# First stage of a hybrid decoder layer: order of loads, norm by token tile, rank of the modulation, place of the transposes

## The chip, the cores and the metric

One core of one Trainium2 chip runs the kernel. The metric is the device time of one execution in microseconds; less is better. The time before is 936.29 us, the median of three runs (935.62 to 937.29). Engines are named as in the profile: PE (TensorE), DVE (VectorE), ACT (ScalarE), POOL (GpSimd), SP (the queue that issues the loads).

## The reference, cut to what matters

512 tokens, width 1024, all in float32. The first stage of the layer computes a conditioned norm and projects it:

```python
mod = (jax.nn.silu(c) @ w_ada + b_ada)[:, None, :]
shift_a, scale_a, gate_a, shift_f, scale_f, gate_f = jnp.split(mod, 6, axis=-1)
h = rms_norm(x, attn_norm) * (1.0 + scale_a) + shift_a
(nq, nkc, nvc, nks, nvs, nkw, nvw, ngate,
 cq, ckv, kr, bgate) = jnp.split(h @ w_in, IN_OFFSETS, axis=-1)
```

Attention over compressed, selected and windowed keys, a second attention (MLA), an output projection and a gated MLP follow; the change leaves their code alone.

## The kernel before, in words

The width is cut into eight blocks `k` of 128 columns, the tokens into four tiles `t` of 128. Every float32 product is made of three matmuls: both operands are split into a high and a low part (`split`, L82: ACT rounds the high part at L83, DVE subtracts at L84), and `mm3` (L87) multiplies high by high, low by high and high by low. `wh`/`wl` are the parts of a weight piece, `hTh`/`hTl` those of the transposed, modulated `h`.

**First stage.** `x` comes in as eight loads (L417). The sum of squares of each half row (L434, L437) gives `rsx`, two token tiles at a time, through POOL (L135). `x_half(i)` scales half of the columns and transposes four blocks `k` into `xnT` (L453, L455). The conditioning vector is a matrix-vector product: `mod_acc(j)` loads eight pieces of `w_ada` (`ada`, 256 KB each, L467), which hold the shifts and the scales of two blocks (a pair `j`, `j+1`), and adds them up on DVE (`acc`, L120 and L122). `mod_cols(j)` sums `acc` over the partitions with two one-column matmuls (operand `onesr`) and makes the columns `mS` and `mA` (L477 to L480). `prep(k)` loads two pieces of `w_in` (408 and 384 columns, `wr`), splits them, and makes `h` of `xnT`, `mS` and `mA` on ACT (L507), then `hTh` and `hTl`. Block `k`'s step of the projection is then 12 matmuls of 408 columns into four banks (`psG`, `psG`, `psS`, `psS`) and 9 of 512 into `psO`, `psF` and a `psT`.

**Second stage.** The four banks of 408 columns are turned into gates (`gt`, `gates`) and a normalized `cqn` for each token tile (L548), which frees the bank. The same four banks and `psF` then take the projection of 320 + 128 further columns (`bB`, `bV1`), block by block. `psF` must first be read by the three instructions L573 to L575 (rotary embedding, output `a`). `X` are the split inputs of the compression, made of `kc`.

**Order.** A scheduler places the instructions on each engine by its own timeline, ranked by a priority (`tc.high_priority`); an engine then takes them in the order in which they stand. `tc.keep_in_program_order` (`pin`) fixes one. Tiles of one tag share a number of buffers (`BIG`, `BANKS`, `bufs`): a load or a matmul into a buffer waits until it has been read out. `W_PRIO` is the rank of the weight splits, `LATE` a list of which small late load goes with which block.

Of the kernel before, what the change touches and what calls it, by code (L numbers as in the profile page):

```python
# [10 lines left out]
F32 = mybir.dt.float32  # L11
# [22 lines left out]
LATE = (0, 1, 1, 1, 2, 2, 2, 3, 3, 4, 5, 6, 7, 8, 9, 9, 9)  # L34
X_ACT = ((0, 0, 1, 1), (1, 1, 1, 1))
# [3 lines left out]
def tile_hybrid_layer(  # L39
# [18 lines left out]
    W_PRIO = [-50]  # L58
# [37 lines left out]
    def raw_unit():  # L96
        return wp.tile([P, 512], F32, name="wr", tag="wr", bufs=5)

    @priority(lambda: W_PRIO[0])
    def load_w(segs, k0, kk, raw=None, tag=None):  # L100
        n = sum(g[2] for g in segs)
        assert kk * n <= 512
        raw = raw_unit() if raw is None else raw
# [5 lines left out]
        rv, hv, lv = (a[:, :kk * n].rearrange("p (k n) -> p k n", k=kk) for a in (raw, wh, wl))  # L109
        at = 0  # L110
        for src, c0, m in segs:
            dma(rv[:, :, at:at + m],
                src[k0 * P:(k0 + kk) * P, c0:c0 + m].rearrange("(k p) n -> p k n", p=P))
            at += m
        split(wh[:, :kk * n], wl[:, :kk * n], raw[:, :kk * n])
        return hv, lv

    def gemv_step(acc, w, k, init):
        if k == 0 and init:
            vec.tensor_scalar(acc, w, csil[:, 0:1], None, op0=ALU.mult)  # L120
        else:
            vec.scalar_tensor_tensor(acc, w, csil[:, k:k + 1], acc, op0=ALU.mult, op1=ALU.add)  # L122
# [286 lines left out]
    with tc.tile_pool(name="p1", bufs=1) as p1:  # L409
# [15 lines left out]
        vec.tensor_scalar(csil, csil, 0.5, None, op0=ALU.mult)  # L425

        ssh = sm.tile([P, NT, 2], F32, name="ssh")
        ssx = sm.tile([P, NT], F32, name="ssx")
        rsx = sm.tile([P, NT], F32, name="rsx")
        for t in range(NT):  # L430
            for i in range(2):
                if i:
                    scr = pj.tile([P, 512], F32, name="scr", tag="t2")
                    vec.tensor_tensor_reduce(scr, xt[t][i], xt[t][i], 1.0, 0.0, ALU.mult, ALU.add, ssh[:, t, i:i + 1])  # L434
                else:
                    scr = pj.tile([P, 512], F32, name="scr", tag="qg")
                    act.activation(scr, xt[t][i], AF.Square, accum_out=ssh[:, t, i:i + 1])  # L437
            if t % 2:
                t2 = slice(t - 1, t + 1)
                vec.tensor_add(ssx[:, t2], ssh[:, t2, 0], ssh[:, t2, 1])  # L440
                rstd(rsx[:, t2], ssx[:, t2], D, [P, 2])
        xnT = []

        def x_half(i):
            for t in range(NT):
                if X_ACT[i][t]:
                    act.activation(xt[t][i], xt[t][i], AF.Copy, scale=rsx[:, t:t + 1])
                else:
                    vec.tensor_scalar(xt[t][i], xt[t][i], rsx[:, t:t + 1], None, op0=ALU.mult)
            for k in range(4 * i, 4 * i + 4):  # L450
                tr = bank("T")
                for t in range(NT):
                    pe.transpose(tr[:, t * P:(t + 1) * P], xt[t][i][:, (k % 4) * P:(k % 4 + 1) * P], ident)  # L453
                xk = slot("KV", f"xnT{k}") if k < 6 else slot("KS", f"xnT{k}")[:, 0:512]
                act.activation(xk, tr, AF.Copy)  # L455
                xnT.append(xk)

        x_half(0)
# [3 lines left out]
        def mod_acc(j):  # L462
            if j % 2 == 0:
                acc = slot("U", "acc")
                for k in range(KD):
                    a = slot("ml", "ada")
                    dma(a.rearrange("p (s n) -> p s n", s=2),  # L467
                        w_ada[k * P:(k + 1) * P, 0:2 * D].rearrange("p (s n) -> p s n", s=2)[:, :, j * P:(j + 2) * P])
                    gemv_step(acc, a, k, True)
                for i in range(2):  # L470
                    ACC[j + i] = [acc[:, s * 256 + i * P:s * 256 + (i + 1) * P] for s in range(2)]

        def mod_cols(j):
            b = bank("T")
# [3 lines left out]
            bp = sm.tile([P, 1], F32, name="bp")  # L478
            vec.scalar_tensor_tensor(bp, b[:, 1:2], 1.0, colA[:, 24 + j:25 + j], op0=ALU.add, op1=ALU.add)
            vec.tensor_mul(mA[:, j:j + 1], bp, colA[:, 8 + j:9 + j])  # L480
# [11 lines left out]
        def late_load(i):  # L492
            for dst, src in late[LATE[i]:LATE[i + 1]]:
                tc.keep_in_program_order(dma(dst, src))

        bA = [bank("G"), bank("G"), bank("S"), bank("S")]
        bF = [bank("O"), bank("F"), None]
        wk = {}

        def prep(k):  # L500
            mod_acc(k)
            mod_cols(k)
            wk[k] = (load_w([(w_in, O_NG, 408)], k, 1, slot("cq", "wr1")),
                     load_w([(w_in, O_KC, 384)], k, 1, slot("cq", "wr2")))
            late_load(k)
            h = pj.tile([P, 512], F32, name="h", tag="t1")
            act.activation(h, xnT[k], AF.Identity, scale=mA[:, k:k + 1], bias=mS[:, k:k + 1])  # L507
            hh, hl = slot("hT", f"hTh{k}", F32R), slot("hT", f"hTl{k}", F32R)
            split(hh, hl, h)
            hTh.append(hh)  # L510
            hTl.append(hl)

        prep(0)
        x_half(1)
        for k in range(KD):
            if k + 1 < KD:
                prep(k + 1)
            if k == 0:
                bF[2] = bank("T")
            hh, hl = hTh[k], hTl[k]  # L520
            (w1h, w1l), (w2h, w2l) = wk[k]
            st, sp = k == 0, k == KD - 1
            for t in range(NT):
                ts = slice(t * P, (t + 1) * P)
                mm3(bA[t][:, 0:408], hh[:, ts], hl[:, ts], w1h[:, 0, :], w1l[:, 0, :], st, sp)
            for i in range(3):
                cs = slice(i * P, (i + 1) * P)
                mm3(bF[i], w2h[:, 0, cs], w2l[:, 0, cs], hh, hl, st, sp)

        tr = bank("T")  # L530
        pe.transpose(tr[:, 0:76], rowsB, ident[0:76, 0:76])
# [7 lines left out]
        for t in range(NT):  # L539
            b = bA[t]  # L540
            act.activation(gt[:, t, :], b[:, 0:24], AF.Tanh, scale=0.5)
            s1 = sm.tile([P, 1], F32, name="s1")
            sq = pj.tile([P, 512], F32, name="sq", tag="t2")
            act.activation(sq[:, 0:384], b[:, 24:408], AF.Square, accum_out=s1)
            r1 = sm.tile([P, 1], F32, name="r1")
            rstd(r1, s1, 384, [P, 1])
            cn = slot("ml", f"cqn{t}")
            vec.scalar_tensor_tensor(cn[:, 0:384], b[:, 24:408], r1, gcq, op0=ALU.mult, op1=ALU.mult)  # L548
            cqn.append(cn)
# [8 lines left out]
        for k in range(KD):  # L558
            wh, wl = load_w([(w_in, O_CKV, 320), (w_in, O_VC + P, P)], k, 1)
            late_load(KD + k)  # L560
# [4 lines left out]
            mm3(bV1, wh[:, 0, 320:448], wl[:, 0, 320:448], hTh[k], hTl[k], st, sp)  # L565

# [550 lines left out]
```

## Time and profile before

| what | value |
|---|---|
| median of three runs | 936.29 us |
| the profiled execution | 936.09 us |
| its span, first to last instruction | 934.1 us |
| PE, DVE, ACT busy | 900.9, 689.3, 511.0 us |
| mean granted TensorE clock | 0.998 |

The profiled execution lies 0.2 us under the median; 2.0 us of it lie outside the span. Times in the rows are microseconds from the span's start. The first projection matmul starts at 22.96, the first stage's last one ends at 63.39, the second stage's at 83.88.

### The profile page before, as it was taken

Reading aid. Unit: us, or ns where it says so; the run is one execution under the profiler, and the core shown is the slowest. Engines: PE = TensorE matmul, PEld = TensorE weight load, DVE = VectorE, ACT = ScalarE, POOL = GpSimd, SP = SyncE. Lnnn points to the kernel's source line nnn. Section 1 sums busy time; section 2 is a strip of 40 time slices with the busy share of each in tenths; the row PEclk is TensorE's granted clock in tenths of the full one; section 3 lists DMA queues with packets and bytes.
Section 4 is the critical chain, followed back from the end, with each engine's and each line's share of the span. In section 5 each row is a group of like instructions: output and inputs, shape, how many; then the busy total and the mean of one; then the engine's idle time right before and its main releaser. Section 6 shows DMA issues by size and latency. Waiting matters only on the chain.

```text
span 934.1 us, 14791 instructions
## 1 busy us (share of the span) xinstructions
PE 900.9 (96%) x5079; PEld 790.9 (85%) x5079; DVE 689.3 (74%) x1505; ACT 511.0 (55%) x1241; POOL 49.9 (5%) x57
## 2 busy tenths in 40 slices
PE   4899999999999999999999999999999999999998
PEld 3899888889899998889898889888888888888886
DVE  7967878798977779688877798797786766722423
ACT  5546868567675657558765764554444444422220
POOL 1000101011000001001011010000000000000000
PEclk9999999999999999999999999999999999999999
DMA  9934672542331263341214354363353333232421
GB/s 299 346 115 140 183 213 83 157 127 54 106 99 35 58 172 102 103 138 35 57 58 147 100 178 118 91 192 91 118 167 99 93 99 101 92 102 91 145 91 46
DMA packets 131682, 113.05 MB, mean 121 GB/s; under 512 B 7515, under 2 KB 110487, under 8 KB 131607
## 3 DMA queue, kind: packets, MB, share of 16 engines
q1 hardware_dynamic: 130838, 110.00, 39.4%
q0 software_dynamic: 768, 2.11, 0.7%
q8 instruction: 40, 0.66, 0.3%
q14 instruction: 36, 0.29, 0.1%
HBM read 109.98 MB, written 2.10 MB: 120 GB/s over the span
## 4 chain that ended last, share of the span: by engine, by line
PE 89%; DVE 4%; ACT 3%; DMA 3%; issue 1%; SPq 0%; DVEq 0%; ACTq 0%
PE psG L87 42%; PE psS L87 24%; PE psO L87 9%; PE psF L87 5%; PE psT L87 4%; PE psT L783 2%; DMA ada<-in_w_ada_dram 2%; DVE wl L84 1%; ACT Pt L760 1%; ACT wh L83 1%; ACT sq L223 1%; DMA x<-in_x_dram 1%; DMA wr<-in_w_in_dram 0%; DVE acc L122 0%; PE psT L808 0%
## 5 line engine op out<-in xcount | busy, mean ns | idle before, releaser
L83 ACT ACTIVATE wh<-wr 128x512 fp32r<-128x512 f32 (+3 forms) x304 | 187.1, 621 | 288.5 <-PE psS L87 104.2
L84 DVE TENSOR_TENSOR wl<-wr,wh 128x512 fp32r<-128x512 f32 (+3 forms) x304 | 203.3, 676 | 158.1 <-ACT wh L83 150.8
L87 PE MATMUL psG<-hTh,wh 128*128 128x512 f32 x192 | 76.5, 399 | 1.0 <-DVE qr L328 1.0
L87 PE MATMUL psG<-hTh,wl 128*128 128x512 f32 x192 | 76.3, 397 | 0.1
L87 PE MATMUL psG<-hTl,wh 128*128 128x512 f32 x192 | 76.3, 397 | 0.0
L87 PE MATMUL psS<-h2l,wh 128*128 128x512 f32 (+1 forms) x184 | 68.2, 371 | 0.0
L87 PE MATMUL psG<-h2h,wl 128*128 128x512 f32 (+1 forms) x184 | 68.2, 371 | 0.0
L87 PE MATMUL psG<-h2l,wh 128*128 128x512 f32 (+1 forms) x184 | 68.1, 371 | 0.0
L87 PE MATMUL psG<-h2h,wh 128*128 128x512 f32 (+1 forms) x184 | 68.1, 372 | 0.0
L87 PE MATMUL psS<-h2h,wl 128*128 128x512 f32 (+1 forms) x184 | 68.0, 371 | 0.0
L87 PE MATMUL psS<-h2h,wh 128*128 128x512 f32 (+1 forms) x184 | 68.0, 371 | 0.0
L760 ACT ACTIVATE Pt<-psS,nm 128x128 f32<-128x128 f32 (+2 forms) x96 | 51.3, 535 | 26.1 <-DVE nm L755 20.1
L122 DVE SCALAR_TENSOR_TENSOR acc<-wr,csil,acc 128x512 f32<-128x512 f32 x60 | 44.8, 747 | 2.9 <-DMA wr<-in_w_ada_dram 1.6
L84 DVE TENSOR_TENSOR PTl<-psT,PTh 128x384 fp32r<-128x384 f32 (+1 forms) x72 | 42.2, 598 | 6.4 <-ACT PTh L83 5.8
L83 ACT ACTIVATE PTh<-psT 128x384 fp32r<-128x384 f32 (+1 forms) x72 | 36.6, 530 | 16.5 <-PE psT L783 16.3
L87 PEld LDWEIGHTS psG<-hTh,wh 128*128 128x128 f32 x192 | 36.2, 188 | 7.6 <-PE psS L87 0.7
L87 PEld LDWEIGHTS psG<-hTh,wl 128*128 128x128 f32 x192 | 36.1, 188 | 7.2 <-DVE wl L84 0.5
L87 PEld LDWEIGHTS psG<-hTl,wh 128*128 128x128 f32 x192 | 36.1, 188 | 6.4
L87 PE MATMUL psG<-wh,hTh 128*128 128x256 f32 (+2 forms) x128 | 38.1, 308 | 3.6 <-ACT wh L83 2.2
L87 PEld LDWEIGHTS psG<-h2l,wh 128*128 128x128 f32 x184 | 34.7, 188 | 6.1
L87 PE MATMUL psG<-wl,hTh 128*128 128x256 f32 (+2 forms) x128 | 38.9, 305 | 0.9 <-DVE wl L84 0.9
L87 PEld LDWEIGHTS psG<-h2h,wh 128*128 128x128 f32 x184 | 34.6, 188 | 6.0
(452 smaller groups left out, 2515.1 us busy)
## 6 DMA issues: line engine op xcount, KB each, us to landing
wr<-in_w_up_dram SPq DMA_DIRECT2D x88, 256.0 KB, 2.9
wr<-in_w_ada_dram SPq DMA_DIRECT2D x64, 256.0 KB, 2.8
wr<-in_w_in_dram SPq DMA_DIRECT2D x48, 256.0 KB, 3.1
wr<-in_w_down_dram SPq DMA_DIRECT2D x44, 256.0 KB, 2.6
ada<-in_w_ada_dram SPq DMA_DIRECT2D x32, 256.0 KB, 5.6
wr<-in_w_o_dram SPq DMA_DIRECT2D x32, 256.0 KB, 3.0
wr<-in_w_in_dram SPq DMA_DIRECT2D x32, 128.0 KB, 2.9
wr<-in_cmp_k_w_dram SPq DMA_DIRECT2D x16, 256.0 KB, 3.3
```

What stands on the lines that cost most here:

```text
L83: act.activation(hi, src, AF.Copy)
L84: vec.tensor_sub(lo, src, f(hi))
L87: ins = pe.matmul(o, lhsT, rhs, start=start, stop=stop, skip_group_check=True)
L122: vec.scalar_tensor_tensor(acc, w, csil[:, k:k + 1], acc, op0=ALU.mult, op1=ALU.add)
L223: act.activation(sq[:, 0:n], b, AF.Square, accum_out=dst)
L760: act.activation(Pt[:, off[x2]:off[x2] + nt[x2]], Sb[x2], AF.Exp, bias=nm[:, x2:x2 + 1], scale=-1.0, accum_out=sums[:, x2:x2 + 1])
L783: pe.transpose(tr[:, e * P:(e + 1) * P], Pt[:, o:o + P], ident)
```

## The change

All loads of the first two stages are pinned in one order on SP: `x` token tile by token tile with the first pieces of `w_ada` between them, the rest of the first pair, `w_in` for blocks 0 and 1, the next pair, `w_in` for the next two blocks, and so on; the small late loads come after the last pair. Each token tile has its own norm, and seven of the eight sums of squares are on ACT. The first four blocks are transposed as their token tile is ready, into four banks (two `psT`, `psO`, `psF`); block 0 is modulated straight out of its bank. `mod_cols`, `x_tile`, `h_split` and the `cqn` loop are ranked 300; the steps are made in pairs. Two DVE instructions for `mA` become one. Cut to its core:

```diff
-LATE = (0, 1, 1, 1, 2, 2, 2, 3, 3, 4, 5, 6, 7, 8, 9, 9, 9)
-X_ACT = ((0, 0, 1, 1), (1, 1, 1, 1))
+LATE = (3, 4, 5, 6, 7, 8, 9, 9, 9)
...
-    W_PRIO = [-50]
+    W_PRIO = [300]
+    pin = tc.keep_in_program_order
...
+        at = 0
         for t in range(NT):
             for i in range(2):
-                dma(xt[t][i], x[t * P:(t + 1) * P, i * 512:(i + 1) * 512])
+                pin(dma(xt[t][i], x[t * P:(t + 1) * P, i * 512:(i + 1) * 512]))
+            for k in range(at, (0, 1, 2, 8)[t]):
+                load_ada(0, k)
+            at = (0, 1, 2, 8)[t]
+        for k in range(2):
+            load_in(k)
...
+        trx = [bank(tag) for tag in ("T", "T", "O", "F")]
+        @priority(lambda: 300)
+        def x_tile(t):
...
+            pool.tensor_tensor(rsx[:, t:t + 1], msx[:, t, 1:2], neghalf, op=ALU.pow)
+            vec.tensor_scalar(xt[t][0], xt[t][0], rsx[:, t:t + 1], None, op0=ALU.mult)
+            act.activation(xt[t][1], xt[t][1], AF.Copy, scale=rsx[:, t:t + 1])
+            for k in range(4):
+                pe.transpose(trx[k][:, t * P:(t + 1) * P], xt[t][0][:, k * P:(k + 1) * P], ident)
...
+        def mod_acc(j, held):
+            acc = slot("U", "acc")
+            for k in range(KD):
+                gemv_step(acc, ada[j, k], k, True, held and k == 0)
...
+            if k:
+                act.activation(h, xnT[k], AF.Identity, scale=mA[:, k:k + 1], bias=mS[:, k:k + 1])
+                split(hh, hl, h)
+            else:
+                act.activation(hh, trx[0], AF.Identity, scale=mA[:, 0:1], bias=mS[:, 0:1])
+                vec.tensor_scalar(h, trx[0], mA[:, 0:1], mS[:, 0:1], op0=ALU.mult, op1=ALU.add)
+                vec.tensor_sub(hl, h, f(hh))
...
+        for j in range(0, KD, 2):
+            if j + 2 < KD:
+                for k in range(KD):
+                    load_ada(j + 2, k)
+                for k in (j + 2, j + 3):
+                    load_in(k)
+                mod_acc(j + 2, True)
+            else:
+                late_load(-1)
...
+            if j + 2 == KD:
+                wB = [load_b(k, 2) for k in range(2)]
+            proj(j)
+            proj(j + 1)
+            if j + 2 < KD:
+                for k in (j + 2, j + 3):
+                    mod_cols(k)
...
+        with tc.high_priority(offset=300):
+            for t in range(NT):
+                b = bA[t]
```

What this makes of the engines' order is shown at three places. The first is DVE at the first modulation. Before:

```order
L122 SCALAR_TENSOR_TENSOR acc<-ada,csil,acc 128x512 x7
L84 TENSOR_TENSOR wl<-wr_232,wh 128x408
L120 TENSOR_SCALAR acc<-ada,csil 128x512
L84 TENSOR_TENSOR wl<-wr_238,wh 128x384
L477 TENSOR_TENSOR mS<-psT,colA 128x1
L479 SCALAR_TENSOR_TENSOR bp<-psT,colA 128x1
```

And of the change:

```order
L139 SCALAR_TENSOR_TENSOR acc<-ada,csil,acc 128x512 x4
L87 TENSOR_TENSOR wl<-wr_143,wh 128x408
L87 TENSOR_TENSOR wl<-wr_144,wh 128x384
L87 TENSOR_TENSOR wl<-wr_147,wh 128x408
L87 TENSOR_TENSOR wl<-wr_148,wh 128x384
L503 TENSOR_TENSOR mS<-psG,colA 128x1
L504 SCALAR_TENSOR_TENSOR mA<-psG,bp_158,colA 128x1
```

The first `mS` stood behind the two weight splits of block 0; it now stands behind those of blocks 0 and 1. The second place is PE where the modulation of later blocks is summed. Before, inside block 3's step:

```order
L87 MATMUL psS<-wh,hTl_424 128x408
L87 MATMUL psT<-onesr,acc 128x1 x2
L87 MATMUL psS<-wh,hTl_424 128x408
L87 MATMUL psO<-hTl_424,wh 128x512
L87 MATMUL psO<-hTh_423,wl 128x512
```

Of the change, between block 1 (`hTh_301`) and block 2 (`hTh_435`); it looks the same between blocks 3 and 4 and between 5 and 6:

```order
L92 MATMUL psF<-hTh_301,wl 128x512
L92 MATMUL psT<-hTl_302,wh 128x512
L92 MATMUL psT<-hTh_301,wl 128x512
L92 MATMUL psT<-onesr,acc 128x1 x4
L92 MATMUL psG<-wh,hTh_435 128x408
L92 MATMUL psG<-wl,hTh_435 128x408
```

The one-column matmuls have moved from inside a step to directly ahead of the step that needs them. The third place is DVE after the last block's `hTl`, where the banks of the first stage are read out. Before:

```order
L548 SCALAR_TENSOR_TENSOR cqn_718<-psG,r_714,qs_113 128x384
L132 TENSOR_SCALAR ms<-s_731 128x1
L573 TENSOR_TENSOR a_946<-psO,tabs 128x512
L548 SCALAR_TENSOR_TENSOR cqn_728<-psG,r_724,qs_113 128x384
L84 TENSOR_TENSOR wl<-wr,wh 128x448
L550 TENSOR_SCALAR gates<-gt 128x4x24
```

Of the change, with the first `cqn` (`cqn_720`) just ahead of the first row shown:

```order
L87 TENSOR_TENSOR wl<-wr,wh 128x448
L628 TENSOR_TENSOR gates<-gates,tabs 128x1
L149 TENSOR_SCALAR ms<-s_733 128x1
L149 TENSOR_SCALAR ms<-s_743 128x1
L652 TENSOR_TENSOR a_935<-psO,tabs 64x512
L653 TENSOR_TENSOR a_935<-psO,tabs 64x512
L608 TENSOR_SCALAR qcol<-colB 128x1
L609 TENSOR_SCALAR gcol<-colB 128x1
L87 TENSOR_TENSOR X<-colB,X 128x16x2
L624 SCALAR_TENSOR_TENSOR cqn_730<-psG,r_726,qs_113 128x384
L624 SCALAR_TENSOR_TENSOR cqn_740<-psS,r_736,qs_113 128x384
L624 SCALAR_TENSOR_TENSOR cqn_750<-psS,r_746,qs_113 128x384
```

The second to fourth `cqn` have moved from among the first `a` to behind all three of its instructions, two weight splits and most of the gates.

## Rows read from the trace of the kernel before

**Rows 1.** The page: busy time of each engine, and the chain of work that ended last by engine.

```profile
PE 900.9 (96%) x5079; PEld 790.9 (85%) x5079; DVE 689.3 (74%) x1505; ACT 511.0 (55%) x1241; POOL 49.9 (5%) x57
...
PE 89%; DVE 4%; ACT 3%; DMA 3%; issue 1%; SPq 0%; DVEq 0%; ACTq 0%
```

**Rows 2.** Busy time by stage. Columns: stretch, its length, then busy time and number of instructions of PE, PEld, DVE, ACT, POOL, the granted TensorE clock, the DMA share and GB/s.

```profile
0.00:22.96 22.96, 9.14 (x38) 6.75 (x38) 16.09 (x43) 13.79 (x27) 2.54 (x8) 1.00 0.92 298
22.96:63.39 40.43, 38.05 (x198) 34.85 (x197) 29.95 (x73) 21.17 (x46) 1.64 (x3) 1.00 0.79 258
63.39:83.88 20.49, 20.16 (x124) 18.89 (x123) 17.36 (x45) 11.31 (x26) 1.38 (x3) 1.00 0.36 102
...
104.00:136.00 32.00, 28.35 (x206) 26.10 (x205) 26.50 (x51) 21.71 (x54) 4.67 (x3) 0.95 0.70 202
```

**Rows 3.** PE in order of time in the first stage. Columns: start, duration, engine, line, operation, output and inputs, shape, count, and in brackets the idle time before and what ended it.

```profile
19.18 4.12 PE L453 MATMUL psT<-ident,x 128*128 128x128 f32 x16
22.96 0.69 PE L87 MATMUL psG<-wh,hTh 128*128 128x408 f32 x1
...
29.54 0.60 PE L87 MATMUL psT<-onesr,acc 128*128 128x1 f32 x4 [0.96 <-DVE bp L479]
...
34.38 0.34 PE L87 MATMUL psG<-wh,hTh 128*128 128x408 f32 x1
...
38.64 0.34 PE L87 MATMUL psG<-wh,hTh 128*128 128x408 f32 x1
...
41.35 0.50 PE L87 MATMUL psT<-onesr,acc 128*128 128x1 f32 x4
...
45.28 0.45 PE L87 MATMUL psG<-wh,hTh 128*128 128x408 f32 x1 [1.41 <-ACT hTh L83]
```

**Rows 4.** The loads: GB/s in slices of 1.25 us from 0 to 50 us, and the DVE instruction that waited for the twentieth load (the second pair's first `ada`).

```profile
GB/s 0 25 231 315 254 293 310 389 380 353 346 351 361 351 333 346 348 351 369 380 363 342 348 350 364 358 382 311 317 357 317 334 359 348 294 315 393 354 344 240
...
18.93 0.49 DVE L120 TENSOR_SCALAR acc<-ada,csil 128x512 f32<-128x512 f32 x1 [0.74 <-DMA ada<-in_w_ada_dram]
```

**Rows 5.** DVE and ACT in order of time: links of the chain from a modulation's sum to `hTh`, and one weight split of 384 columns.

```profile
18.13 0.51 ACT L83 ACTIVATE wh<-wr 128x384 fp32r<-128x384 f32 x1
...
43.77 0.80 ACT L507 ACTIVATE h<-xnT,mS,mA 128x512 f32<-128x512 f32 x1
44.59 0.63 ACT L83 ACTIVATE hTh<-h 128x512 fp32r<-128x512 f32 x1
...
53.80 0.82 ACT L507 ACTIVATE h<-xnT,mS,mA 128x512 f32<-128x512 f32 x1 [2.65 <-DVE mA L480]
```

**Rows 6.** DVE in order of time, first and second stage.

```profile
19.33 0.55 DVE L84 TENSOR_TENSOR wl<-wr,wh 128x384 fp32r<-128x384 f32 x1
...
41.92 0.15 DVE L477 TENSOR_TENSOR mS<-psT,colA 128x1 f32<-128x1 f32 x1
41.99 0.15 DVE L479 SCALAR_TENSOR_TENSOR bp<-psT,colA 128x1 f32<-128x1 f32 x1
...
53.54 0.16 DVE L480 TENSOR_TENSOR mA<-bp,colA 128x1 f32<-128x1 f32 x1
...
62.35 0.68 DVE L573 TENSOR_TENSOR a<-psO,tabs 128x512 f32<-128x512 f32 x1
62.95 0.61 DVE L548 SCALAR_TENSOR_TENSOR cqn<-psG,r,qs 128x384 f32<-128x384 f32 x1
63.47 0.61 DVE L84 TENSOR_TENSOR wl<-wr,wh 128x448 fp32r<-128x448 f32 x1
...
64.83 0.69 DVE L574 TENSOR_TENSOR a<-psO,tabs 64x512 f32<-64x512 f32 x1
...
71.20 1.98 DVE L84 TENSOR_TENSOR X<-kc,X 128x496 fp32r<-128x496 f32 x2
```

**Rows 7.** PE in order of time, second stage.

```profile
63.39 0.23 PE L531 MATMUL psT<-ident,rowsB 76*128 76x76 f32 x1
63.42 0.39 PE L87 MATMUL psG<-wh,hTh 128*128 128x320 f32 x1
63.65 0.31 PE L87 MATMUL psG<-wl,hTh 128*128 128x320 f32 x1
...
71.22 0.50 PE L87 MATMUL psF<-hTh,wh 128*128 128x512 f32 x1 [0.33 <-DVE a L575]
...
74.08 0.45 PE L87 MATMUL psG<-wh,hTh 128*128 128x320 f32 x2
...
83.65 0.39 PE L87 MATMUL psF<-hTh,wl 128*128 128x512 f32 x1
```

**Rows 8.** ACT in order of time, second stage.

```profile
73.42 0.58 ACT L83 ACTIVATE wh<-wr 128x448 fp32r<-128x448 f32 x1 [0.16 <-PE psF L87]
74.10 2.09 ACT L83 ACTIVATE X<-kc 128x496 fp32r<-128x496 f32 x2
```

**Rows 9.** Busy time and granted clock around 110 us, columns as in rows 2, and ahead of them the wait of PE there.

```profile
107.75 0.50 PE L87 MATMUL psG<-wh,hTh 128*128 128x256 f32 x2 [1.00 <-ACT wh L83]
...
108.00:110.00 2.00, 1.65 (x9) 1.44 (x9) 2.00 (x4) 2.00 (x3) 0.00 (x0) 0.73 0.35 87
110.00:112.00 2.00, 2.00 (x12) 2.00 (x11) 2.00 (x4) 2.00 (x9) 0.00 (x0) 0.50 0.73 224
112.00:114.00 2.00, 2.00 (x18) 2.00 (x18) 2.00 (x5) 1.15 (x3) 0.88 (x1) 0.92 0.03 8
```

More of the change, by code (lines that the diff above doesn't have):

```diff
@@ L108, in load_w, with gemv_step @@
             wl = wp.tile([P, 512], F32R, name="wl", tag="wl", bufs=4)
[L109 to L115, printed above, removed]
+        hv, lv = (a[:, :kk * n].rearrange("p (k n) -> p k n", k=kk) for a in (wh, wl))
+        split(wh[:, :kk * n], wl[:, :kk * n], raw[:, :kk * n], held)
         return hv, lv
[L118 removed]
+    def gemv_step(acc, w, k, init, held=False):
         if k == 0 and init:
[L120 removed]
+            ins = vec.tensor_scalar(acc, w, csil[:, 0:1], None, op0=ALU.mult)
+            if held:
+                pin(ins)
         else:
@@ L414, in tile_hybrid_layer, with load_ada, load_in @@
         dma(rowsA, vec_a)
+        ada, raws = {}, {}
+        G1, G2 = [(w_in, O_NG, 408)], [(w_in, O_KC, 384)]
+        def load_ada(j, k):
+            a = slot("ml", "ada")
+            pin(dma(a.rearrange("p (s n) -> p s n", s=2),
+                    w_ada[k * P:(k + 1) * P, 0:2 * D].rearrange("p (s n) -> p s n", s=2)[:, :, j * P:(j + 2) * P]))
+            ada[j, k] = a
+        def load_in(k):
+            raws[k] = [slot("cq", f"wr{i}") for i in range(2)]
+            for r, g in zip(raws[k], (G1, G2)):
+                load_raw(r, g, k, 1)
+        at = 0
         for t in range(NT):
             for i in range(2):
-                dma(xt[t][i], x[t * P:(t + 1) * P, i * 512:(i + 1) * 512])
+                pin(dma(xt[t][i], x[t * P:(t + 1) * P, i * 512:(i + 1) * 512]))
[4 more added lines that the diff above has]
+            load_in(k)
         tr = bank("T")
@@ L458, in tile_hybrid_layer @@
-        x_half(0)
-        ACC = {}
[L462 to L471, printed above, removed]
+            vec.tensor_scalar(msx[:, t, 0:1], ssh[:, t, 0:1], 1.0 / D, EPS, op0=ALU.mult, op1=ALU.add)
@@ L473, in mod_cols @@
+        ACC = {}
+        def mod_acc(j, held):
+            acc = slot("U", "acc")
+            for k in range(KD):
+                gemv_step(acc, ada[j, k], k, True, held and k == 0)
+            for i in range(2):
+                ACC[j + i] = [acc[:, s * 256 + i * P:s * 256 + (i + 1) * P] for s in range(2)]
+        @priority(lambda: 300)
         def mod_cols(j):
-            b = bank("T")
+            b = bank("G" if j < 2 else "T")
             for s in range(2):
@@ L477, in mod_cols, with x_keep, x_half1 @@
             vec.tensor_add(mS[:, j:j + 1], b[:, 0:1], colA[:, 16 + j:17 + j])
-            bp = sm.tile([P, 1], F32, name="bp")
-            vec.scalar_tensor_tensor(bp, b[:, 1:2], 1.0, colA[:, 24 + j:25 + j], op0=ALU.add, op1=ALU.add)
-            vec.tensor_mul(mA[:, j:j + 1], bp, colA[:, 8 + j:9 + j])
+            vec.scalar_tensor_tensor(mA[:, j:j + 1], b[:, 1:2], bp1[:, j:j + 1], colA[:, 8 + j:9 + j],
+                                     op0=ALU.add, op1=ALU.mult)
+        for t in range(NT):
+            x_tile(t)
+        mod_acc(0, False)
+        for j in range(2):
+            mod_cols(j)
+        xnT = [None]
+        def x_keep(k, tr):
+            xk = slot("KV", f"xnT{k}") if k < 7 else slot("KS", f"xnT{k}")[:, 0:512]
+            act.activation(xk, tr, AF.Copy)
+            xnT.append(xk)
+        def x_half1(k0, k1):
+            for k in range(k0, k1):
+                tr = bank("T")
+                for t in range(NT):
+                    pe.transpose(tr[:, t * P:(t + 1) * P], xt[t][1][:, (k % 4) * P:(k % 4 + 1) * P], ident)
+                x_keep(k, tr)
         rowsB = p1.tile([76, P], F32, name="rowsB")
@@ L492, in late_load, with w_split, h_split, load_b @@
         def late_load(i):
[L493 to L497, printed above, removed]
+            for dst, src in late[0 if i < 0 else LATE[i]:LATE[i + 1]]:
+                pin(dma(dst, src))
         wk = {}
[L500 to L505, printed above, removed]
+        def w_split(k):
+            wk[k] = [load_w(g, k, 1, r) for g, r in zip((G1, G2), raws[k])]
+        @priority(lambda: 300)
+        def h_split(k):
             h = pj.tile([P, 512], F32, name="h", tag="t1")
-            act.activation(h, xnT[k], AF.Identity, scale=mA[:, k:k + 1], bias=mS[:, k:k + 1])
             hh, hl = slot("hT", f"hTh{k}", F32R), slot("hT", f"hTl{k}", F32R)
-            split(hh, hl, h)
+            if k:
[5 more added lines that the diff above has]
+                vec.tensor_sub(hl, h, f(hh))
             hTh.append(hh)
             hTl.append(hl)
[L513 to L519, printed above, removed]
+        def load_b(k, held=0):
+            return load_w([(w_in, O_CKV, 320), (w_in, O_VC + P, P)], k, 1, held=held)
+        def proj(k):
             hh, hl = hTh[k], hTl[k]
@@ L528, in tile_hybrid_layer @@
                 mm3(bF[i], w2h[:, 0, cs], w2l[:, 0, cs], hh, hl, st, sp)
+        wB = []
+        for j in range(0, KD, 2):
[5 more added lines that the diff above has]
+                mod_acc(j + 2, True)
+            else:
+                late_load(-1)
+            if j == 0:
+                w_split(0)
+                h_split(0)
+                for k in range(1, 4):
+                    x_keep(k, trx[k])
+                w_split(1)
+                h_split(1)
+                x_half1(4, 8)
+                bA = [bank("G"), bank("G"), bank("S"), bank("S")]
+                bF = [bank("O"), bank("F"), bank("T")]
+            else:
+                for k in (j, j + 1):
+                    w_split(k)
+                    h_split(k)
+            if j + 2 == KD:
[5 more added lines that the diff above has]
+                    mod_cols(k)
         tr = bank("T")
-        pe.transpose(tr[:, 0:76], rowsB, ident[0:76, 0:76])
+        pin(pe.transpose(tr[:, 0:76], rowsB, ident[0:76, 0:76]))
         vec.tensor_copy(colB, tr[:, 0:76])
@@ L538, in tile_hybrid_layer @@
         cqn, ckvn = [], []
[L539 to L549, printed above, removed]
+        with tc.high_priority(offset=300):
+            for t in range(NT):
+                b = bA[t]
+                act.activation(gt[:, t, :], b[:, 0:24], AF.Tanh, scale=0.5)
+                s1 = sm.tile([P, 1], F32, name="s1")
+                sq = pj.tile([P, 512], F32, name="sq", tag="t2")
+                act.activation(sq[:, 0:384], b[:, 24:408], AF.Square, accum_out=s1)
+                r1 = sm.tile([P, 1], F32, name="r1")
+                rstd(r1, s1, 384, [P, 1])
+                cn = slot("ml", f"cqn{t}")
+                vec.scalar_tensor_tensor(cn[:, 0:384], b[:, 24:408], r1, gcq, op0=ALU.mult, op1=ALU.mult)
+                cqn.append(cn)
         vec.tensor_scalar(gates.rearrange("p g t -> p t g"), gt, 0.5, 0.5, op0=ALU.mult, op1=ALU.add)
```

72 lines of the change are left out of this document (37 added, 35 removed).

## The prediction

> **What bounds the kernel now.** I read the page first. PE is busy 96% of the span and the chain that ended last runs through PE for 89% of it [rows 1]: a gain has to come out of stretches where PE waits or starts late, and a loss is whatever makes PE wait anew. The change touches the first two stages, so I cut the span there [rows 2]. Up to 22.96 PE does only transposes and sums and the loads run at 298 GB/s; that is the one stretch where PE is late. From 22.96 to 63.39 PE is busy 38.05 of 40.43 us, and from 63.39 to 83.88 it is busy 20.16 of 20.49: both stages are already PE's. From 104 to 136 PE idles 3.65 us.
>
> Next I read PE in order of time [rows 3]. One block's step takes 4.26 us (34.38 to 38.64), eight take 34.1; the other 6.3 us of the stage are one-column sums and waits such as the 0.96 us at 29.54 and the 1.41 us at 45.28. So a new first stage can win by starting before 22.96, and by having less than 6.3 us beside its steps.
>
> **The start of the projection.** In both kernels the first pair's modulation rests on the same 17 loads (one small, eight of `x`, eight `ada`), 33 KB and sixteen times 262 KB, 4.23 MB, so mixing `x` and `ada` cannot bring its last piece earlier. What decides is what stands ahead of the first `mS` on DVE: now four weight splits, so four pieces of `w_in`, the last of which ends at 5.04 MB. Before, a load that ended at 4.93 MB was waited for until 18.93 [rows 4]; 0.11 MB more at 348 GB/s is 0.3 us, so it lands at 19.2. Then ACT's high part 0.51 [rows 5], DVE's low part 0.55, `mS` and 0.07 later `mA` for 0.16 [rows 6], 0.10 to ACT (53.70 to 53.80, [rows 5, 6]), and one instruction of the form 0.82 [rows 5] that makes block 0's `hTh` from its bank: with small hand-overs 21.5. That is **1.5 us earlier** than 22.96 [rows 3]. Bounds: 20.1, if the piece is there as soon as 5.04 MB have moved (17.8 by the slices of [rows 4]); 22.5, if ACT, which also evicts four banks just before, is a microsecond late.
>
> The other edits ahead of this point I cost at nothing: the sums of squares moved to ACT, the norm by tile, the folded `mA` all end while DVE waits for the 19.2 load. If DVE were late instead, each 0.7 us of its work would delay the start by as much; the 22.5 holds that.
>
> **The length of the first stage.** The eight steps stay: 34.1 us. Two things are added on PE.
>
> First, eight of the sixteen transposes of the second half now stand inside block 0's step; before, all sixteen ran ahead of the first projection, 4.12 us for the sixteen [rows 3]. Eight are 2.1 us. Bounds 1.9 to 2.3 (the same rows).
>
> Second, the three boundaries between pairs. The one-column sums now stand directly ahead of the step whose `hTh` needs them, so PE waits out the whole chain: sum to `mS` 0.57 (41.35 to 41.92, [rows 3, 6]), `mA` 0.07 later for 0.16 [rows 6], 0.10 to ACT, `h` to `hTh` 0.82 (43.77 to 44.59) and `hTh` 0.63 [rows 5], 0.06 to PE (45.22 to 45.28, [rows 3]): 2.4 us each. Three make 7.2 us. `acc` itself is ready before (DVE begins its eight accumulations at 20.6; they and some five splits, at 0.6 to 0.7 each, end near 30, and the boundary is at about 32), so PE's place, not the data, sets the wait, and DVE and ACT stand idle ahead of it too. Lower bound 1.0 each, the wait of the same kind at 29.54; upper 2.9, if a weight split of 0.5 gets ahead.
>
> 34.1 + 2.1 + 7.2 = 43.4 us against 40.43: the first stage ends at 64.9 instead of 63.39, **1.5 us later**. The start gained is given back twice.
>
> The loads do not set this. All of them up to the last pair's `w_in` are 13.76 MB, which at the rates of [rows 4] end near 43 to 45. Pinned behind one another on SP, four `ada` of the last pair also wait for accumulations that follow the first boundary; that may hold SP some 3 us, and its sixteen later loads with it. The last boundary comes at about 21.5 + 10.6 + 2 x (2.4 + 8.5) = 54, so cover of 6 us is left; without it the stage would be late by what the loads lack.
>
> **The second stage.** I count from the end of the first, E. PE's row takes the four banks one after another, four blocks each (12 matmuls), then `psF`. A bank is free when its `cqn` has run. Before, the second `cqn` ran at 62.95, ahead of E [rows 6], and PE went from 63.42 through 48 such matmuls to `psF` at 71.22, waiting 0.33 us [rows 7]: about 0.15 us each.
>
> In the change each block's high-by-low matmuls come last in its step, so the four banks are complete only some six matmuls of 0.23 ahead of E, and DVE can begin the gates at E - 0.7. Ahead of the second `cqn` stand: one `a` 0.60 and a `cqn` 0.52 (start to start), two weight splits 1.04, two `a` of 64 partitions 1.38 [rows 6], and some fifteen small instructions at about 0.08 apart, 1.2. With itself (0.6) it ends at E + 4.7. PE has used up the first bank long before and waits; the remaining 36 matmuls take 5.4, so `psF` starts at E + 10.1 instead of E + 7.8. The third and fourth `cqn` and the reads of `psF` (four `a` or `kc` and two `cqn`, 3.7 us) are done by E + 8.5 and lie under this.
>
> After `psF` (2.86 us, 71.22 to 74.08, [rows 7]) the next block needs its high part, and on ACT that now stands behind the second `kc`'s two `X` copies. DVE reaches that `kc` after two `X` of its own (1.98, [rows 6]), at about E + 11.1; ACT's two copies take 2.09 and the high part 0.58 [rows 8]: E + 13.8 against PE's E + 13.0. 0.8 us more. Together **3.2 us**, after which the last four blocks take 9.8 us as before (74.08 to 83.88). Lower bound 0, if the evictions keep ahead as they did; upper 5, if the splits of the later blocks fall behind the four `X` too.
>
> The two transposes and a few small DVE rows for later stages move behind 100 us; they are under 0.3 us each where PE waits anyway.
>
> **Sum.** -1.5 + 3.0 + 3.2 = +4.7 us on the profiled execution's 936.09; the median of the runs lies 0.2 higher, so 941.0.
>
> **The clock, weighed.** After PE waits of 1.00 and 0.35 us near 107, the granted clock fell to 0.50, the 1.2 GHz level, and rose again by 114 [rows 9]: 0.54 + 1.00 + 0.16 us lost, 1.7. After the wait of 1.41 us at 45.28 it stayed at 1.00 [rows 2, 3]. The new waits are longer, 1.9 us idle at a boundary and over 2 in the second stage. The Trainium skill ("TensorE: Matmul & The Clock Gate", Part 1: The HAM clock gate) says that an idle PE falls back to 1.2 GHz and that activity releases it; it speaks against this change, and by it, with a fall at each of the three boundaries, the time would be 946.1. The sum above goes by the row at 45.28, no fall.
>
> **Rivals.**
> *The clock falls in the new waits.* For it [rows 9], against it the 1.41 us wait. One fall is 1.7 us, three 5.1: 942.7 to 946.1. 22%.
>
> *Stage three swallows the delay (the other side).* From 104 to 136 PE idles 3.65 us and loses 1.7 to the clock [rows 2, 9], in waits on loads and weight splits. If those loads run on their own time while PE arrives later, up to 5.3 us of delay vanishes there: 941.0 - 5.3 = 935.7. It decides against my forecast from about 2.8 us on. Against it: the loads there go into a few buffers that splits have to free, and the splits wait for PE, so they come later by as much. 14%.
>
> *The evictions keep pace.* If the scheduler's order in the second stage costs nothing, only the first stage's 1.5 us stay: 937.8. For it, PE waited 0.33 us there before [rows 7]; against it, the place of the second `cqn`. 12%.
>
> *The change does what it says.* If the first `mS` ran right behind the sums, at about 18, the start would be near 19 and the total 938.5. The order excludes it, and I give it no chance of its own.
>
> **How the numbers follow.** The forecast itself, 939.0 to 943.0, has 52%. A measurement of this kernel can tell about 0.2%, 1.9 us, from no change: faster is under 934.4, slower over 938.2. Slower: the forecast, the clock, and a little of the others, 0.74. Same: half of stage three's case and most of the evictions', 0.15. Faster: stage three's case where the evictions keep pace too, 0.11. The range takes the low bounds of the boundaries (4.2 us less) with stage three's half, 934.5, and two falls of the clock with the upper bound of the second stage, 946.5.
>
> **What would show it.** In the profile after: the first projection matmul at 21 to 22; three PE waits of some 2 us ended by `hTh`, at about 32, 43 and 54; the first stage's end near 65; in the second stage PE waits ended by `cqn` and by `wh`, `psF` ten microseconds behind the first stage's end, and the stage's end near 88.5. The steps are wrong if those waits are shorter or the third stage is shorter than before. The whole is wrong if PE's stretch from the start of projection to 88 is not longer than before's 60.9.

## The result, and the profile after

The changed kernel takes 947.47 us (median of four runs, 947.23 to 947.84) beside 935.98 us of the kernel before on the same chip: a ratio of 1.0121, 95% interval 1.0103 to 1.0138, **11.5 us slower**. The forecast was 941.0 us with a range of 934.5 to 946.5. The direction was right, the size was not: the loss is more than twice the 4.7 us of the sum, and just outside the range. One execution of the run with the last step pinned, below, took 1506.5 us at a granted clock of 0.56, and that run's figures leave it out.

The stages of the changed kernel, cut where [rows 2] cut those of before; the fourth stretch is the third stage shifted by the delay at its start. Columns as there.

```profile
0.00:21.95 21.95, 8.73 (x33) 6.17 (x33) 13.78 (x42) 13.56 (x30) 3.40 (x10) 1.00 0.92 298
21.95:69.85 47.90, 43.88 (x200) 39.60 (x201) 31.27 (x62) 20.93 (x41) 0.55 (x1) 0.93 0.70 224
69.85:93.85 24.00, 20.57 (x122) 18.53 (x121) 18.24 (x46) 12.14 (x32) 2.47 (x5) 1.00 0.30 87
114.00:146.00 32.00, 27.91 (x211) 25.21 (x210) 26.86 (x57) 21.82 (x55) 5.88 (x3) 1.00 0.68 204
```

The start is 1.0 us earlier, the first stage 7.5 us longer (40.43 before), the second 3.5 us longer (20.49). In the first stage PE is not only idle for 4.0 us; its *busy* time grew by 5.8 us, at a mean granted clock of 0.93. That is the part that the sum did not have. PE in order of time shows the start, the first boundary between pairs, the other two, and the stage's end:

```profile
21.95 0.71 PE L92 MATMUL psG<-wh,hTh 128*128 128x408 f32 x1 [0.36 <-ACT hTh L553]
22.46 0.55 PE L92 MATMUL psG<-wl,hTh 128*128 128x408 f32 x1
22.80 0.55 PE L92 MATMUL psG<-wh,hTh 128*128 128x408 f32 x1
...
25.69 1.22 PE L523 MATMUL psT<-ident,x 128*128 128x128 f32 x8
26.67 0.61 PE L92 MATMUL psG<-wh,hTl 128*128 128x408 f32 x2
...
33.38 0.50 PE L92 MATMUL psT<-onesr,acc 128*128 128x1 f32 x4
34.26 0.61 PE L92 MATMUL psT<-onesr,acc 128*128 128x1 f32 x4 [0.38 <-DVE mA L504]
35.82 0.45 PE L92 MATMUL psG<-wh,hTh 128*128 128x408 f32 x1 [0.96 <-ACT hTh L84]
...
46.02 0.50 PE L92 MATMUL psT<-onesr,acc 128*128 128x1 f32 x4
...
48.47 0.46 PE L92 MATMUL psG<-wh,hTh 128*128 128x408 f32 x1 [0.96 <-ACT hTh L84]
...
58.74 0.50 PE L92 MATMUL psT<-onesr,acc 128*128 128x1 f32 x4
...
61.19 0.46 PE L92 MATMUL psG<-wh,hTh 128*128 128x408 f32 x1 [0.96 <-ACT hTh L84]
...
69.85 0.23 PE L606 MATMUL psT<-ident,rowsB 76*128 76x76 f32 x1
```

Each boundary, from the sums to the next `hTh` matmul, takes 2.44 to 2.45 us; of this the rows count 0.38 and 0.96 us as idle, less than the 1.9 us that the prediction named. Between them lie the pairs of steps: 11.43, 10.20, 10.27 and 8.66 us. A pair should take 8.52 (two of the 4.26 us of [rows 3]), the first about one more for its transposes. The windows behind the boundaries say why the second and third do not:

```profile
36.00:38.00 2.00, 2.00 (x8) 1.96 (x9) 1.97 (x4) 0.97 (x2) 0.00 (x0) 0.58 0.93 284
38.00:40.00 2.00, 2.00 (x7) 1.70 (x6) 1.97 (x4) 0.48 (x1) 0.00 (x0) 0.57 0.87 276
40.00:42.00 2.00, 2.00 (x12) 1.77 (x11) 1.96 (x4) 0.81 (x2) 0.00 (x0) 1.00 0.95 300
...
50.00:52.00 2.00, 2.00 (x7) 1.68 (x6) 1.93 (x4) 1.08 (x2) 0.00 (x0) 0.50 0.83 252
52.00:54.00 2.00, 2.00 (x8) 1.74 (x8) 1.97 (x4) 0.54 (x1) 0.00 (x0) 0.66 0.88 257
...
62.00:64.00 2.00, 2.00 (x12) 1.86 (x11) 0.59 (x1) 1.34 (x2) 0.00 (x0) 1.00 0.00 0
```

Behind the first two boundaries the granted clock falls to the 1.2 GHz level and PE, busy all the time, gets through 7 or 8 instructions in 2 us instead of 12. Behind the third, equally long, it does not fall.

The second stage, PE in order of time, answers to [rows 7]:

```profile
70.78 0.38 PE L92 MATMUL psG<-wh,hTh 128*128 128x320 f32 x1 [0.70 <-DVE cqn L624]
...
74.91 0.39 PE L92 MATMUL psG<-wh,hTh 128*128 128x320 f32 x1 [2.03 <-DVE cqn L624]
...
80.26 0.39 PE L92 MATMUL psF<-hTh,wh 128*128 128x512 f32 x1
...
83.86 0.56 PE L92 MATMUL psG<-wh,hTh 128*128 128x320 f32 x2 [0.70 <-ACT wh L84]
```

`psF` stands 10.4 us behind the first stage's end, and behind it PE waits 0.70 us for `wh`: the two waits that the prediction named, within 0.3 us of its figures.

### The profile page after: what moved, and what is told of

It reads as the page before. It is cut to its first block, busy times and chain, and to the rows that moved or that the text cites. A ratio compares the mean times of both kernels' runs of the same rounds, so it can differ in the third digit from the quotient of the medians.

```text
span 945.2 us, 14794 instructions
## 1 busy us (share of the span) xinstructions
PE 906.9 (96%) x5079; PEld 793.6 (84%) x5079; DVE 689.9 (73%) x1499; ACT 511.0 (54%) x1243; POOL 52.0 (6%) x59
## 4 chain that ended last, share of the span: by engine, by line
PE 82%; ACT 3%; DVE 3%; DMA 1%; issue 1%; SPq 0%; DVEq 0%; ACTq 0%
PE psG L92 40%; PE psS L92 23%; PE psO L92 8%; PE psF L92 4%; PE psT L92 3%; PE psT L861 2%; DVE wl L87 1%; DMA wr<-in_w_in_dram 1%; ACT wh L84 1%; ACT Pt L838 1%; DMA wr<-in_cmp_k_w_dram 0%; ACT sq L240 0%; PE psF L373 0%; PE psT L886 0%; PE psT L1024 0%
## 5 line engine op out<-in xcount | busy, mean ns | idle before, releaser
L92 PEld LDWEIGHTS psG<-hTh,wh 128*128 128x128 f32 x192 | 36.2, 188 | 7.6 <-PE psS L92 0.7
L92 PEld LDWEIGHTS psG<-hTl,wh 128*128 128x128 f32 x192 | 36.2, 188 | 6.4
L92 PEld LDWEIGHTS psG<-h2h,wl 128*128 128x128 f32 x184 | 34.6, 188 | 6.0
```

Source lines behind the costliest of these rows:

```text
L92: ins = pe.matmul(o, lhsT, rhs, start=start, stop=stop, skip_group_check=True)
```

## The experiments

The theory after the result: two clock falls behind boundary waits are the missing 3.4 us of the first stage; boundaries, second stage and start are as the sum had them. Five runs take one thing each, four combine. Ratios are to the kernel before, with their 95% interval.

### Boundary waits filled with work that adds nothing

```diff
                 for k in (j + 2, j + 3):
                     mod_cols(k)
+                    for _ in range(5):
+                        mm(bA[3][:, 0:408], zr, hTh[j + 1][:, 0:408], False, False, True)
```

The operand `zr` is zero, and the sums are pinned too, so that the order holds.

> The order and the waits of the changed kernel stay, but at each boundary PE gets five more matmuls of 408 columns behind the first pair of sums and five behind the second; their stationary operand is zero, so they add nothing to the bank. Ten at 0.185 us are 1.85 us, nearly all of the 2.44 us. Theory (PE's idle time in the boundary is what makes the clock fall behind it): boundaries stay at 2.4 to 2.7 us, the second and third pair fall from 10.2 to 8.6 us, granted clock 1.00 from 36 to 54, the time 944. Rival (the slow pairs have nothing to do with PE's idle time): pairs stay at 10.2, the time 947.5 or a little more.

Measured: 946.0 us, 1.0103 (1.0085 to 1.0121). PE at the second boundary, and two windows of the same run, the whole first stage and two microseconds of the second:

```profile
44.54 0.50 PE L92 MATMUL psT<-onesr,acc 128*128 128x1 f32 x4
44.90 1.17 PE L92 MATMUL psS<-hTh,zr 128*128 128x408 f32 x5
...
47.28 0.35 PE L92 MATMUL psG<-wh,hTh 128*128 128x408 f32 x1
```

```profile
22.00:67.12 45.12, 45.12 (x230) 41.83 (x231) 31.08 (x62) 20.96 (x41) 0.55 (x1) 1.00 0.75 236
...
74.00:76.00 2.00, 2.00 (x10) 2.00 (x9) 1.94 (x4) 2.00 (x4) 0.00 (x0) 0.50 0.00 0
```

The boundaries became longer (2.74 us), yet the second and third pair fell to 8.56 and 8.55 us and the stage from 47.90 to 45.12. With PE busy in the waits the granted clock is 1.00 through the stage: PE's idling there is the cause of the falls, and their price is 3.4 us (10.20 + 10.27 - 8.56 - 8.55). The other executions agree: the four of this run read a mean granted clock of 0.998 to 1.00, the changed kernel's four 0.996. The time gained less, since now the wait of 2.04 us on `cqn` in the second stage was followed by a fall (the last row), where the changed kernel had none behind its 2.03 us.

### The last step pinned

```diff
-            proj(j + 1)
+            proj(j + 1, j + 2 == KD)
```

The new argument pins that step's matmuls.

> Only the last step of the first stage is pinned in program order: its four banks psG and psS are complete 2.1 us before the stage's end (nine matmuls of 512 columns follow) instead of at its end. Theory (the second stage is longer because the gates' reads of the banks begin only at the end of the first): psF starts 7.5 to 8 us behind the end of the first stage instead of 10.4, no PE wait on cqn over 0.5 us, second stage 20.5 to 21, the time 944. Rival (the splits and the rotary reads on DVE set the second stage, not the place of the banks): the PE wait moves to wl, wh or a, stage 23 to 24, the time 947. The first stage itself should stay at 47.9 within 0.3.

Measured: 943.55 us (median of three), 1.0078 (1.0061 to 1.0095). PE at the stage's end and at `psF`, two rows of DVE, and the busy time of the second stage:

```profile
69.58 0.23 PE L606 MATMUL psT<-ident,rowsB 76*128 76x76 f32 x1
...
76.87 0.50 PE L92 MATMUL psF<-hTh,wh 128*128 128x512 f32 x1
```

```profile
68.29 0.61 DVE L624 SCALAR_TENSOR_TENSOR cqn<-psG,r,qs 128x384 f32<-128x384 f32 x1
68.82 0.68 DVE L651 TENSOR_TENSOR a<-psO,tabs 128x512 f32<-128x512 f32 x1
```

```profile
69.58:89.53 19.95, 19.95 (x122) 18.67 (x121) 16.78 (x40) 11.19 (x26) 1.39 (x3) 1.00 0.38 105
```

`psF` stands 7.3 us behind the stage's end, and there is no wait in the second stage at all, 19.95 us. The pin took away the whole of the second stage's loss. It did so in two ways at once: the four banks are complete earlier, and the scheduler gave DVE another order with it, the second `cqn` at 68.29 ahead of the first `a` instead of at 74.15 behind all three. Which of the two would have been enough this run does not show. The second stage ends 4.3 us earlier than in the changed kernel, and 3.8 us of that arrive at the end of the span.

### Both together

The edits of the two runs above.

> The boundary waits filled with zero matmuls and the last step pinned, both together. Filled waits alone gained 3.0 us up to the end of the second stage's wait on cqn and then a clock fall at 74 to 78 took about 1.7 us back. Theory (that fall belongs to the wait of 2.04 us on cqn): with the last step pinned there is no such wait and no fall, the two gains add up, first stage 45.1 us, second 20.0, the time 940 to 941. Rival (a fall comes somewhere in this stretch whatever is done): granted clock under 0.9 somewhere from 24 to 90, the time 942 to 943.

Measured: 940.51 us, 1.0046 (1.0033 to 1.0059). The stages:

```profile
21.98:67.34 45.36, 45.36 (x231) 42.04 (x232) 32.44 (x67) 22.18 (x45) 1.64 (x3) 1.00 0.76 237
67.34:87.25 19.91, 19.91 (x123) 18.67 (x121) 16.82 (x40) 11.21 (x26) 1.39 (x3) 1.00 0.37 105
```

PE is busy without a gap from 21.98 to 87.25 and the clock stays at 1.00. The two gains add up, and the fall of the filled run belonged to the wait on `cqn`.

### The sums early

```diff
+                for j in mid if t == 1 else ():
+                    mod_cols(j)
...
-            proj(j + 1)
-            if j + 2 < KD:
-                for k in (j + 2, j + 3):
-                    mod_cols(k)
+            proj(j + 1, more, (j + 2, j + 3) if more else ())
```

> The sums of the next pair's modulation stand six matmuls into the pair's second step (which is pinned in program order for it) instead of behind the pair. The accumulations they need were done 3.6 to 3.9 us ahead of each boundary in the profile of the changed kernel, so nothing new is waited for. Theory (the boundary waits, and the two clock falls that follow them, are 7.3 + 3.4 us of the first stage): each boundary is under 0.4 us, no pair takes more than 9.0 us except the first, the granted clock stays at 1.00 from 36 to 60, first stage 38 to 39 us instead of 47.9, the time 937 to 938. Rival (the slow second and third pair, 10.2 us instead of 8.5, have another cause, such as loads that run at the same time): the boundaries go but the pairs stay at 10.2, first stage 41.5, the time 941. Rival (the loads bind as soon as the stage is shorter): waits on wh behind a load at the last pair.

Measured: 940.86 us, 1.0046 (1.0031 to 1.0062). PE at the sums of the third pair, and the windows behind them:

```profile
40.88 0.61 PE L92 MATMUL psT<-onesr,acc 128*128 128x1 f32 x4 [0.58 <-DVE acc L139]
41.87 0.61 PE L92 MATMUL psT<-onesr,acc 128*128 128x1 f32 x4 [0.38 <-DVE mA L504]
```

```profile
42.00:44.00 2.00, 2.00 (x11) 1.98 (x12) 1.45 (x5) 1.36 (x2) 0.00 (x0) 0.78 0.79 171
44.00:46.00 2.00, 2.00 (x7) 1.52 (x6) 2.00 (x4) 1.88 (x3) 0.00 (x0) 0.50 0.93 358
```

The boundary waits on `hTh` are gone, but the stage shrank only to 43.72 us where 38 to 39 were expected. Each group of sums still takes PE 1.34 us (30.21 to 31.55 at the first), not under 0.4. And "nothing new is waited for" was wrong: with PE faster, DVE is late with the third pair's accumulations (it waited 0.32 us for a load itself), and this wait of 0.58 us, with the 0.38 behind it, was followed by a fall of its own. That order also made the second stage 20.56 us.

### The first sum ahead of block 1's splits

```diff
-                w_split(1)
+                w_split(1, 2)
```

The new argument pins both parts of the split.

> Block 1's weight splits are pinned behind block 0's hl, so that the first mS on DVE stands behind two weight splits instead of four. Theory of the prediction (these splits, and the load behind the last of them, set the start of the projection): mS at 19.8, ACT has the first hTh at 20.7 to 20.9, the first projection matmul at 20.8 to 21.0 instead of 21.95, the time 946.4. Rival (PE sets it itself: the sums run to 20.50 and four transposes stand between them and the first projection matmul, until 21.5): the first projection matmul at 21.5 to 21.6, the time 947. In both the first ten matmuls still run at the half pace (0.34 us for 408 columns).

Measured: 947.08 us, 1.0112 (1.0094 to 1.0130). PE there:

```profile
18.75 1.87 PE L92 MATMUL psG<-onesr,acc 128*128 128x1 f32 x8 [0.53 <-DVE acc L139]
20.47 1.09 PE L523 MATMUL psT<-ident,x 128*128 128x128 f32 x4
21.37 0.71 PE L92 MATMUL psG<-wh,hTh 128*128 128x408 f32 x1
```

The rival is right: the first `mS` ran at 20.22, 0.6 us earlier, but the eight one-column sums take 1.72 us and the four transposes behind them 0.90, so PE itself starts the projection no earlier than 21.4.

### PE's idle time ahead of the projection filled

```diff
             x_tile(t)
+            for _ in range((7, 16, 10, 2)[t]):
+                mm(wb[:, 0:P], zr, zr, True, True, True)
```

The transposes are pinned with them.

> The changed kernel with PE's idle time ahead of the projection filled: 7, 16, 10 and 2 matmuls of 128 columns by a zero operand, into a bank that is not read, behind the transposes of the four token tiles (pinned). They fit into waits of 0.85, 1.97, 1.26 and 0.26 us. Theory (the first ten projection matmuls run at the half pace, 0.34 us instead of 0.185 for 408 columns, because PE idled before, though the granted clock is recorded as 1.00 there): the one-column sums shrink from 1.7 us, the first projection matmul stays at 21.6 to 21.9 (the weight splits on DVE), the first ten matmuls run at 0.185 to 0.23, the first pair takes 9.5 to 10.0 us instead of 11.4, the time 945.7 to 946. Rival (the pace there has another cause, such as the loads at 350 GB/s): 0.34 stays, the first pair stays at 11.4, the time 947.5.

Measured: 945.1 us (944.5 to 947.9), 1.0100 (1.0086 to 1.0115), not to be told from the changed kernel with certainty. The trace is that of the execution of 947.9 us; the other three, 944.5 to 945.7, read a mean granted clock of 0.998 instead of 0.996, and what went otherwise in them no trace shows. Busy time ahead of the projection, and PE at its start:

```profile
8.00:21.54 13.54, 13.40 (x64) 13.01 (x64) 10.41 (x27) 8.95 (x19) 2.14 (x3) 1.00 1.07 358
```

```profile
21.54 0.71 PE L92 MATMUL psG<-wh,hTh 128*128 128x408 f32 x1
22.04 0.55 PE L92 MATMUL psG<-wl,hTh 128*128 128x408 f32 x1
22.38 0.55 PE L92 MATMUL psG<-wh,hTh 128*128 128x408 f32 x1
```

My theory fell in this trace: PE was busy 13.4 of 13.5 us, and the first projection matmuls still stand 0.34 us apart (0.43 for the two of 512 columns). Early idling alone is not the cause of the half pace. What filled the time were transposes, one-column sums and products of zeros; whether such work counts as much as the projection's no run here shows.

### Combinations

The first takes the early sums (one bank for a pair's), the early start and the pinned last step; the second step of every pair is pinned in it.

> Three edits of the single runs together: the sums early (behind the third token tile of the pair's second step, those of both blocks into one bank, so that the second block's do not wait for the first's mA), block 1's weight splits behind the first mS, and the last step pinned. Theory: start at 21.4, the first pair 12.3 (half pace at its start, sums), the second and third 9.3 each with no wait over 0.3 us and no clock fall, the last 8.6, end of the first stage at 61, second stage 20 us, the time 934 to 935.5, a little under the kernel before. Rival (DVE binds: eight accumulations, four weight splits and two hl are 9.6 us of a pair's 9.3, as the wait of 0.58 us on acc in the run with the early sums shows): waits on acc of 0.5 to 1 us in the second and third pair with a fall of 1.7 us behind each, the time 938 to 940.

Measured: 937.26 us, 1.0014 (1.0006 to 1.0023). There is no clock fall up to 83, and the second stage takes 19.91 us, but the first ends at 63.40 instead of 61: PE waited on `acc` 0.86, 0.41 and 0.43 us, and started at 22.01, since the first `mS` waited for eight sums in one bank. DVE in order of time, at the first `mS` of two pairs:

```profile
32.10 0.16 DVE L504 TENSOR_TENSOR mS<-psT,colA 128x1 f32<-128x1 f32 x1 [1.21 <-PE psT L92]
...
42.23 0.16 DVE L504 TENSOR_TENSOR mS<-psT,colA 128x1 f32<-128x1 f32 x1 [1.14 <-PE psT L92]
```

Between its two waits for the sums DVE works without a gap, 9.0 us (42.23 - 1.14 - 32.10); with 1.14 for the sums that is the pair's 10.1 us. DVE binds, as the rival had it, by this ring and not by 9.6 us of work, and without the falls that it feared. The same with the early filling:

> The combination of the last run with PE's early idle time filled too. Theory of the half pace by idling: the one-column sums ahead of the projection end about 0.8 us earlier, the first projection matmul stands at 20.5 to 20.8 instead of 21.4, the first pair is 1.7 us shorter, so 2.3 to 2.6 us under the combination without it: 932 where that is 934.5. Rival (the half pace has another cause): no difference to the combination.

Measured: 937.23 us, 1.0016 (1.0008 to 1.0025), no difference, and in its trace the half pace lasts to 24.5 us, as in the run without the filling (24.4). This bears out the last section. Then DVE was relieved:

```diff
+            if held == 2:
+                pin(act.activation(acc, w, AF.Copy, scale=csil[:, 0:1]))
```

> The combination of early sums, early start and pinned last step, with two things more against what bound it: the first accumulation of the third and fourth pair goes from DVE (0.48 us) to ACT, and the sums of the first pair keep a bank for each block, so that the first mS waits for four one-column matmuls instead of eight. Theory (DVE's 9.6 us of work in a pair of 9.3 us set the waits on acc of 0.86, 0.41 and 0.43 us): start 21.4 instead of 22.0, waits on acc in the second and third pair under 0.1 us, end of the first stage at 61.5 to 62 instead of 63.4, the second stage 20 us, the time 935 to 936, no measurable difference from the kernel before (936). Rival (the loads bind there, DVE only shows it): the waits stay or move to ACT behind a load, end at 63, the time 937.

Measured: 935.94 us, 1.0001 (0.9992 to 1.0010). PE at the sums, and at the stage's end:

```profile
31.12 1.02 PE L92 MATMUL psT<-onesr,acc 128*128 128x1 f32 x8 [1.45 <-DVE acc L142]
...
40.88 0.95 PE L92 MATMUL psT<-onesr,acc 128*128 128x1 f32 x8
...
50.30 0.95 PE L92 MATMUL psT<-onesr,acc 128*128 128x1 f32 x8
...
62.33 0.23 PE L610 MATMUL psT<-ident,rowsB 76*128 76x76 f32 x1
```

The second and third wait on `acc` are gone, so the ring through DVE had set them; the first, where the accumulations stayed on DVE, grew to 1.45 us. The loss of the change is undone, and no run is faster than the kernel before. The second stage ends at 82.2 here, 1.6 us ahead of the kernel before; 1.2 us of this are lost again up to 150 of before's time and 0.65 behind 804, so an earlier end of these stages is not yet an earlier end of the kernel.

## Why the prediction was wrong in size

**The start**: 21.5 predicted, 21.95 measured, inside the bounds of 20.1 to 22.5. The four splits did set it, but not through the load. ACT and DVE of the changed kernel:

```profile
18.77 0.61 ACT L516 ACTIVATE xnT<-psT 128x512 f32<-128x512 f32 x1
19.25 0.97 ACT L84 ACTIVATE wh<-wr 128x408 fp32r<-128x408 f32 x2
...
20.81 0.15 DVE L503 TENSOR_TENSOR mS<-psG,colA 128x1 f32<-128x1 f32 x1
```

The last of the four pieces had landed at 18.6, not 19.2; ACT, still evicting a bank, rounded the last two from 19.25 to 20.2. That is the case of the upper bound, by half a microsecond, and the near hit of 21.5 is partly luck. PE's own limit of 21.4, which the sum did not see, is only 0.6 us earlier than the measured start.

**The length of the first stage**: 43.4 predicted, 47.9 measured. The three boundaries were right, 7.34 for 7.2 us. The pairs were not: 40.56 for 36.2 us. Of the 4.4 us, 3.4 are the clock behind two boundaries. 0.8 are the first pair: its first ten matmuls took 3.74 us (21.95 to 25.69) where the pace of [rows 3] gives 1.9, while its eight transposes, behind these, took 0.98 instead of the 2.1 that I had read from the slow ones before the projection.

**The clock, weighed**, is the step that failed. It took "no fall" from one wait of 1.41 us in [rows 2, 3], put the falls at nothing in the sum and left them to a rival of 22%; measured, they cost 3.4 us. That rival was the case, with two falls, and its price of 1.7 us each was right (1.68 and 1.75). The second error of the same kind is the first pair: the sum had its first step at full pace. The Trainium skill ("TensorE: Matmul & The Clock Gate", Part 1: The HAM clock gate) says that an idle PE falls back to 1.2 GHz; the trace agrees behind two boundaries (granted 0.57 and 0.50) and not behind the third, as idle as they were. One wait without a fall was evidence that a fall can fail to come, and I used it as evidence that it would not.

**The second stage**: +3.2 predicted, +3.5 measured, with the second `cqn` where the prediction had put it (done 4.9 us behind the first stage's end, 4.7 predicted); the run with the pinned last step, which moved the banks and that `cqn` together, took the loss away.

**Stage three**, the rival on the other side: it swallowed nothing. The delay was 9.97 us at the second stage's end and 10.5 us at 115 of before's time; PE is busy 27.91 of 32 us there beside 28.35 in [rows 2], without a fall of the clock. The last 0.65 us came after 804 of before's time in every kernel made from the changed one; in the changed one 35 matmul rows there lie 0.24 or 0.25 us apart, in the kernel before 4, most of the others 0.22 or 0.23 in both. The cause is open.

With the falls (3.4), the first pair (0.8), the start (0.5), the second stage (0.3) and the 1.1 us behind it, plus 0.3 in the steps and boundaries, the 4.7 us become 11.1, the difference of the two spans. The bounds of the range, added up as the prediction names them, are 934.2 and 946.2, not 934.5 and 946.5; the measured time lies above either.

## What to carry to other kernels

A wait of PE is to be priced with what it does to the clock behind it: here 2.4 us of boundary cost 4.1 when a fall came, and one wait that came off without a fall says little about the next. A sum placed directly ahead of the matmuls that need its result makes PE wait out the whole chain; look at where its inputs were done (3.6 to 3.9 us earlier here) and move it up, but then read what binds next, here DVE's 9.0 us of work between two sums. Where the next stage reads several banks, finish these banks first and let others come last: pinning one step, with the order on DVE that came with it, was worth 4.05 us of a stage.

## What was not expected of the hardware

In the kernels made from the changed one, the first matmuls of 408 columns stand 0.34 us apart, 0.185 later, with a granted clock shown as 1.00 in both. By the Trainium skill ("TensorE: Matmul & The Clock Gate", Part 1, "Wait — 56ns, not 53.3ns?") the spacing at 1.2 GHz is the columns over the clock, by estimate 0.340 us here; the rows agree. The trace's own clock entries begin only at 26.1 us in the changed kernel, 23.6 in the kernel before and 24.4 in the first run under Combinations, each time where the pace changes: for the stretch ahead the view has no entry and shows 1.00. The same part has activity raise the clock; the run with the filled start does not bear this out for the work that filled it, with PE busy 13.4 of 13.5 us ahead of the projection. In the kernel before, the half pace fell mostly on transposes. What ends it no run here shows.

Nor do the waits say which one a fall follows: 0.38 and 0.96 us in a boundary, twice yes and once no; 2.03 us no and 2.04 us yes; 0.58 and 0.38 us around a few one-column sums, yes; 1.41 us in the kernel before and 1.45 us in the last combination, no. As far as the mean granted clock tells, it differs between executions of one kernel too: with the first sum ahead, three read a mean granted clock of 0.996 and the one of 945.06 us read 0.998.
